# A hybrid attention block on one core: 32 unused bytes ahead of the activations

## The chip, the cores and the metric

The kernel runs on one core of a Trainium2 chip. The time is that of one execution on the device in microseconds; three runs of the kernel before are given by their median, lowest and highest. A profile of one execution stands beside them, with the start and the duration of every instruction.

## What is computed

One decoder block over 512 tokens of width 1024, all in float32, batch 1. Two token mixers run side by side on the same normalised input, their gated results are merged, and a SwiGLU layer follows:

```python
h = rms_norm(x, norm_mix_pre[l])
proj = h @ w_in[l]
(g_q, g_k, g_v, g_r, g_a, n_q, n_kc, n_vc, n_ks, n_vs, n_kw, n_vw,
 n_gate, merge_gla, merge_nsa) = jnp.split(proj, split_points, axis=-1)
o_gla = gla_mixer(g_q, g_k, g_v, g_r, g_a, ...)
o_nsa = nsa_mixer(n_q, n_kc, n_vc, n_ks, n_vs, n_kw, n_vw, n_gate, ...)
mixed = (jax.nn.sigmoid(merge_gla) * (o_gla @ w_proj_gla[l])
         + jax.nn.sigmoid(merge_nsa) * (o_nsa @ w_proj_nsa[l]))
x = x + rms_norm(mixed @ w_out[l], norm_mix_post[l])
h = rms_norm(x, norm_ffn_pre[l])
f = (jax.nn.silu(h @ w_ffn_gate[l]) * (h @ w_ffn_up[l])) @ w_ffn_down[l]
x = x + rms_norm(f, norm_ffn_post[l])
```

`gla_mixer` is a chunked gated linear attention of 4 heads, `nsa_mixer` a sparse attention of 8 heads with a compressed, a selected and a sliding-window branch. The hidden width of the SwiGLU layer is 2816.

## The kernel before

**Products.** Nearly all of the work is dense products of weights with activations that are held transposed, 128 features by 512 tokens to a tile. To keep float32 accuracy at the faster fp32r rate, each operand is split in a high and a low part, both fp32r, and a product is three matmuls into one accumulator: high weights with high activations (line 243), high weights with low activations (line 248), low weights with high activations (line 249). These three lines stand in the helper `three`, which all products with transposed activations share. The weights are the stationary operand, 128x128 to a matmul, and the activations stream past them as the moving operand, so each of the three matmuls has a weight load ahead of it that overlaps with the matmul before (PEld in the profile). The first projection, of line 569, goes the other way: the activations (`hu`) are stationary and the weights move, 440 columns at a time.

**Widths.** Plain products move 512 columns. Pairs of products, and the units of SwiGLU and of the down projection, use a seven-product scheme (as Strassen's) on halves of the tokens and move 256 columns. Line 569 moves 440.

**Stages, in the order of time.** Line 569 projects to the token-major values up to 69 us; then the other projections, woven with GLA, to 245 us; compression and attention with pieces of dense products as filling to 425 us; the output projection to 480 us; SwiGLU to 705 us; the plain part of the down projection to 753 us, the rest of it to the end.

**Where tiles lie.** All on-chip buffers come from pools. A pool of the left side grows upwards from the base, a pool of the right side downwards from the top. The pool `base` is the first on the left: identity, ones, two constants, the norm vectors, then `hT_hi` and `hT_lo` (the activations, 16 KB a partition each) and the eight slots `b0` to `b7`. The other left pools (`mid`, `glat`, `nsa`, `att`, `ffn` and so on) are stacked above it and hold further activations and those weight forms that are sums of weights (`s`, `a22`, the slots `d_two`, `c_two`, `w_uu`, `w_rw` and the like). On the right lie the raw weights as they come from memory (`wraw`) and the ring: two high and two low tiles of 1024 columns, `whi` and `wlo`, through which the other split weights pass, and the softmax tiles. Sizes are rounded up to 32 bytes.

What stands before `hT_hi` adds up to 512 + 512 + 64 + 32 + 32 + 160 = 1312 bytes, 20.5 times 64, from byte 16,512 on, which is 258 times 64. So `hT_hi` starts at byte 17,824, which is 32 mod 64, and since nearly all tiles above it have sizes that are multiples of 128, nearly all of the left side starts at 32 mod 64, as does the right side.

The kernel has earlier devices that set such starts. `half_line` puts 64 bytes into the pool `mid` (line 404), the ring can be opened with a shift of 64 bytes (lines 95 and 131), and the forms of the down projection are shifted by 192 bytes (line 1737). As a result, where 256 columns are moved, the moving operand starts at 32 mod 128 and the weights at 96, 64 bytes apart. Where 512 columns are moved, 613 matmuls with the weights in the ring have both at 32, and 332 have them at 32 and 96. In line 569 the weights move: the two parts of 440 columns in a tile start at 96 and, 1760 bytes further, at 64 mod 128, and the stationary `hu` at 96. Another device is `restart` (line 236), after which the first 256-column product has its middle matmul split in two halves of 128 columns (line 244).

**Order.** Each engine's order follows from the order in which the code issues, and from the waits that the pools set where a buffer is reused. The down projection and the SwiGLU units alternate between weights in the ring and weights in left-side slots.

Of the kernel before, what the change touches and what calls it, by code (L numbers as in the profile page):

```python
# [8 lines left out]
F32 = mybir.dt.float32  # L9
# [141 lines left out]
def hybrid_block_kernel(ctx: ExitStack, tc: tile.TileContext, I, outT):  # L151
# [3 lines left out]
    base = ctx.enter_context(tc.tile_pool(name="base", bufs=1, reuse_waits="tile"))  # L155
# [11 lines left out]
    def bank(tag):  # L167
        return psum.tile([128, 512], F32, tag=tag, bufs=2, name="ps_" + tag)
# [17 lines left out]
    act.activation(out=warm, in_=mhalf[:, 0:1], func=AF.Exp)  # L186
    vecs = base.tile([128, 4 * KD + HG + 2], F32, name="vecs")
    act.dma_start(vecs, I["vecs"])
    spin = bank("acc")
    for i in range(8):  # L190
        pe.matmul(spin[:, 0:128], ones, ones, start=True, stop=True)
# [1866 lines left out]
```

## Time and profile before

| | |
|---|---|
| timed runs | 836.05, 835.23, 834.75 us; median 835.23 us |
| span of the profiled execution, first to last instruction | 833.8 us |
| granted clock of TensorE over the span | 0.997 |
| PE busy | 823.1 us in 5553 matmul records |
| DVE, ACT, POOL busy | 633.1, 526.2, 147.2 us |
| read from and written to memory | 102.21 MB, 4.19 MB |

The profiled execution has no time of its own beside its span; the runs' median lies 1.4 us above the span. How to read the rows: a timeline row gives start and length in us, engine, line, operation, output tile <- input tiles, and the shape. A matmul's recorded length (0.28 us for 256 columns, 0.39 us for 512) includes the time that it takes to pass through the array and overlaps with the next; the step from one start to the next is what a matmul costs in a dense stream.

### The profile page before, as it was taken

The numbers are of one execution on the slowest core, as the hardware profiler recorded it, in microseconds if no ns is written. First come the engines' busy times: TensorE is split into PE (matmuls) and PEld (weight loads), VectorE is DVE, ScalarE is ACT, GpSimd is POOL, SyncE is SP. The second block draws the span as 40 slices with busy tenths as digits, with TensorE's granted clock in tenths as the row PEclk, the third lists the DMA queues.
The fourth block names the chain that finished last, engine by engine and source line by source line (L and its number), as shares of the span: only waits on it lengthen the run. The fifth ranks groups of instructions, "written<-read, shape, count | busy, mean of one in ns | idle before, by whom it ended". The sixth has DMA issues, their size and how long they took to land.

```text
span 833.8 us, 14626 instructions
## 1 busy us (share of the span) xinstructions
PE 823.1 (99%) x5553; PEld 749.7 (90%) x5553; DVE 633.1 (76%) x1198; ACT 526.2 (63%) x973; POOL 147.2 (18%) x176
## 2 busy tenths in 40 slices
PE   9999999999999999999999999999999999999996
PEld 8998899998788787888888999999999999889996
DVE  7765897883377888777666488998888778839985
ACT  6557767763454889887645587766665657535542
POOL 0101022230030000100000365111211110001354
PEclk9999999999999999999999999999999999999998
DMA  8333465762252454454228758789878883325333
GB/s 295 98 110 102 120 121 129 168 145 84 76 182 51 105 127 101 102 127 106 73 76 280 227 153 228 141 209 236 187 187 200 201 182 86 91 77 178 89 103 101
DMA packets 41239, 117.85 MB, mean 141 GB/s; under 512 B 4716, under 2 KB 7036, under 8 KB 41040
## 3 DMA queue, kind: packets, MB, share of 16 engines
q1 hardware_dynamic: 27952, 82.49, 31.9%
q0 software_dynamic: 12496, 33.88, 22.0%
q8 instruction: 43, 0.70, 0.3%
q10 hardware_dynamic: 720, 0.54, 0.2%
q14 instruction: 28, 0.23, 0.1%
HBM read 102.21 MB, written 4.19 MB: 128 GB/s over the span
## 4 chain that ended last, share of the span: by engine, by line
PE 88%; DVE 5%; ACT 4%; POOL 2%; issue 1%; POOLq 0%; DVEq 0%; ACTq 0%
PE ps_mm L243 13%; PE ps_mm L249 13%; PE ps_mm L248 13%; PE ps_sc L243 5%; PE ps_sc L249 5%; PE ps_sc L248 4%; PE ps_acc L248 3%; PE ps_acc L249 3%; PE ps_acc L243 3%; PE ps_tp L249 2%; PE ps_tp L243 2%; PE ps_tp L248 2%; PE ps_tp L569 2%; PE ps_sc L569 2%; PE ps_tp L1139 2%
## 5 line engine op out<-in xcount | busy, mean ns | idle before, releaser
L78 ACT CAST whi<-wraw 128x1024 fp32r<-128x1024 f32 (+2 forms) x62 | 60.2, 973 | 64.9 <-PE ps_mm L248 22.7
L243 PE MATMUL ps_mm<-hT_hi,whi 128*128 128x512 f32 (+1 forms) x260 | 100.1, 385 | 0.2 <-ACT whi L78 0.2
L249 PE MATMUL ps_mm<-hT_hi,wlo 128*128 128x512 f32 (+1 forms) x260 | 97.1, 374 | 0.0
L248 PE MATMUL ps_mm<-hT_lo,whi 128*128 128x512 f32 (+1 forms) x259 | 96.7, 374 | 0.0
L85 DVE TENSOR_TENSOR wlo<-wraw,whi 128x1024 fp32r<-128x1024 f32 (+2 forms) x47 | 51.4, 1096 | 27.0 <-ACT whi L78 26.9
L243 PEld LDWEIGHTS ps_mm<-hT_hi,whi 128*128 128x128 f32 x260 | 48.9, 188 | 10.2 <-ACT whi L78 0.9
L249 PEld LDWEIGHTS ps_mm<-hT_hi,wlo 128*128 128x128 f32 x260 | 48.8, 188 | 9.3 <-DVE wlo L85 0.3
L248 PEld LDWEIGHTS ps_mm<-hT_lo,whi 128*128 128x128 f32 x259 | 48.7, 188 | 7.5
L1462 ACT CAST d_two<-s 128x1024 fp32r<-128x1024 f32 x26 | 27.0, 1044 | 30.5 <-PE ps_mm L249 15.0
L274 DVE TENSOR_TENSOR pl<-ps_tp,ph 128x512 fp32r<-128x512 f32 (+1 forms) x64 | 31.2, 490 | 13.2 <-ACT ph L273 12.5
L1469 DVE TENSOR_TENSOR d_two<-s,d_two 128x1024 fp32r<-128x1024 f32 x25 | 30.6, 1223 | 11.2 <-ACT d_two L1462 10.9
L82 POOL DMA_DIRECT2D wlo<-wraw x15 | 12.8, 852 | 147.3 <-ACT wlo L81 71.3
L1101 ACT ACTIVATE p<-p,mx 128x512 f32<-128x512 f32 (+3 forms) x64 | 35.7, 559 | 4.6 <-DVE mx L1099 4.2
L1099 DVE CUSTOM_DVE_ANT_0 p<-ps_sc,causal 128x512 f32<-128x512 f32 (+3 forms) x64 | 30.0, 488 | 9.5 <-PE ps_sc L1093 8.6
L273 ACT CAST ph<-ps_tp 128x512 fp32r<-128x512 f32 (+1 forms) x64 | 26.6, 417 | 4.4 <-PE ps_tp L1139 3.4
L1838 POOL TENSOR_TENSOR y<-y,us 128x256 f32<-128x256 f32 x12 | 16.0, 1361 | 72.1 <-DVE us L1835 72.1
L1139 PE MATMUL ps_tp<-ident,p 128*128 128x128 f32 x160 | 27.7, 272 | 0.0
L1139 PEld LDWEIGHTS ps_tp<-ident,p 128*128 128x128 f32 x160 | 20.8, 140 | 7.2 <-ACT pc L1023 0.4
L1446 POOL DMA_DIRECT2D wlo<-in_w_gate x13 | 11.5, 887 | 76.8 <-ACT wlo L1444 76.7
L1462 ACT CAST c_two<-s 128x1024 fp32r<-128x1024 f32 x12 | 12.5, 1044 | 18.7 <-PE ps_acc L249 9.5
L243 PE MATMUL ps_mm<-hT_hi,d_two 128*128 128x256 f32 x80 | 22.3, 279 | 0.0
L249 PE MATMUL ps_mm<-hT_hi,d_two 128*128 128x256 f32 x80 | 22.3, 279 | 0.0
(841 smaller groups left out, 3214.6 us busy)
## 6 DMA issues: line engine op xcount, KB each, us to landing
wraw<-in_w_t SPq DMA_DIRECT2D x36, 512.0 KB, 3.9
wraw<-in_w_gate SPq DMA_DIRECT2D x21, 512.0 KB, 4.5
rw<-in_w_up SPq DMA_DIRECT2D x19, 512.0 KB, 8.3
wlo<-wraw POOLq DMA_DIRECT2D x15, 512.0 KB, 4.5
wlo<-in_w_gate POOLq DMA_DIRECT2D x13, 512.0 KB, 8.6
w_uu<-in_w_up POOLq DMA_DIRECT2D x19, 256.0 KB, 8.7
wraw<-in_w_tok SPq DMA_DIRECT2D x11, 440.0 KB, 3.4
wraw<-in_w_proj SPq DMA_DIRECT2D x8, 512.0 KB, 3.6
```

The lines of the kernel that those rows point to most:

```text
L78: self.cast = self.nc.scalar.copy(hi[:, :cols], raw[:, :cols])
L85: self.nc.vector.tensor_tensor(out=lo[:, :cols], in0=raw[:, :cols], in1=hi[:, :cols].bitcast(F32), op=OP.subtract)
L243: pe.matmul(o, wh, xh, start=start, stop=False, skip_group_check=True)
L248: pe.matmul(o[:, c], wh, xl[:, c], start=False, stop=False, skip_group_check=True)
L249: return pe.matmul(o, wl, xh, start=False, stop=stop, skip_group_check=True)
L274: dve.tensor_tensor(out=lo, in0=src, in1=hi.bitcast(F32), op=OP.subtract)
L569: pe.matmul(o, x[:, k, t], y[:, w], start=(k == 0 and m == 0), stop=(k == KD - 1 and m == 2))
L1099: dve.tensor_tensor_reduce(out=o, in0=s, in1=causal[:, S - 128 * (i + 1):S], scale=-1.0, scalar=-NEG, op0=OP.add, op1=OP.min, accum_out=mx ...
L1101: act.activation(out=o, in_=o, func=AF.Exp, scale=-1.0, bias=mx[:, i:i + 1], accum_out=z[:, i:i + 1])
L1139: pe.transpose(tp[:, i * 128:(i + 1) * 128], p[:, OFF[i] + k * 128:OFF[i] + (k + 1) * 128] if i else p0, ident)
L1462: act.copy(hi, t)
L1469: dve.tensor_tensor(out=lo, in0=t, in1=hi.bitcast(F32), op=OP.subtract)
```

## The change

After the norm vectors and ahead of `hT_hi`, one buffer of 8 float32 values a partition is allocated in the pool `base`. Nothing reads or writes it.

```diff
     vecs = base.tile([128, 4 * KD + HG + 2], F32, name="vecs")
     act.dma_start(vecs, I["vecs"])
+    base.tile([128, 8], F32, name="line")
     spin = bank("acc")
```

`hT_hi` starts at byte 17,856 instead of 17,824, and all later left-side tiles move by the same 32 bytes. Their starts of 32 mod 128 become 64, those of 96 become 0. The right side stays where it is, at 32 mod 64. The engines have the same instructions in the same order, with the same waits.

| columns | operands | moving, weights mod 128 before | after | matmuls |
|---|---|---|---|---|
| 256 | both on the left | 32, 96 | 64, 0 | 2116 |
| 256 | moving left, weights in the ring | 32, 96 | 64, 96 | 1222 |
| 512 | moving left, weights in the ring | 32, 32 | 64, 32 | 613 |
| 512 | moving left, weights in the ring | 32, 96 | 64, 96 | 332 |
| 440 | moving in the ring, `hu` on the left | 96, 96 and 64, 96 | 96, 0 and 64, 0 | 288 |

## The prediction

> **What bounds the kernel now.** I read the head of the page first, then the granted clock, then the chain that ended last, and then the starts of single matmuls in the timeline, since the change can only act on how fast an instruction reads or writes its operands.
>
> ```profile
> span 833.8 us, 14626 instructions
> PE 823.1 (99%) x5553; PEld 749.7 (90%) x5553; DVE 633.1 (76%) x1198; ACT 526.2 (63%) x973; POOL 147.2 (18%) x176
> PE 88%; DVE 5%; ACT 4%; POOL 2%; issue 1%; POOLq 0%; DVEq 0%; ACTq 0%
> ```
> ```profile
> core 0: 833.8 us, clock 0.997
> ```
>
> PE is busy for 823.1 of 833.8 us, at a granted clock of 0.997, and it is 88% of the chain. All other waits together leave PE idle for 833.8 - 823.1 = 10.7 us. So the time is the sum of the PE's steps from one matmul to the next, and a change that alters this step by 1% alters the kernel by nearly 1%.
>
> The table by stretches shows that it holds in the two long parts where the other engines have most to do.
>
> ```profile
> 590.00:700.00 110.00, 110.00 (x973) 110.00 (x972) 87.75 (x155) 68.10 (x106) 17.93 (x21) 1.00 0.78 179
> 708.00:752.00 44.00, 44.00 (x191) 35.44 (x190) 28.47 (x44) 22.51 (x39) 0.00 (x0) 1.00 0.27 80
> ```
>
> After the time come PE, PEld, DVE, ACT, POOL, the granted clock, and DMA. In the SwiGLU units (590 to 700) PE has no gap, DVE is busy for 87.75 of 110 us and ACT for 68.10. If PE became 6% faster there, 103.5 us would be left, still more than DVE's 87.75: no other engine would take over.
>
> **The step of a matmul.** The fp32r matmuls have three widths, and the timeline shows what a step of each takes. First 256 columns wide, in one stretch and in another, the first and the last row of 19 each, so 18 steps:
>
> ```profile
> 619.81 0.28 PE L243 MATMUL ps_mm<-x5h,w_uu 128*128 128x256 f32 x1
> ...
> 621.85 0.28 PE L243 MATMUL ps_mm<-x,d_two 128*128 128x256 f32 x1
> ```
> ```profile
> 546.77 0.28 PE L249 MATMUL ps_mm<-x5h,w_uu 128*128 128x256 f32 x1
> ...
> 548.89 0.28 PE L248 MATMUL ps_tp<-hT_lo,d_two 128*128 128x256 f32 x1
> ```
>
> 2.04 us over 18 is 113.3 ns, and 2.12 us over 18 is 117.8 ns. Both stretches have the same starts of their operands (moving at 32, weights at 96 mod 128). So there is a short and a long step, and the start alone doesn't decide which.
>
> Then 512 columns wide, ten rows or nine steps each; in the first pair moving and weights both start at 32 mod 128, in the second the weights start at 96:
>
> ```profile
> 451.73 0.39 PE L248 MATMUL ps_mm<-hT_lo,whi 128*128 128x512 f32 x1
> ...
> 453.77 0.39 PE L248 MATMUL ps_mm<-hT_lo,whi 128*128 128x512 f32 x1
> ```
> ```profile
> 719.76 0.39 PE L243 MATMUL ps_mm<-hT_hi,whi 128*128 128x512 f32 x1
> ...
> 721.86 0.40 PE L243 MATMUL ps_mm<-hT_hi,whi 128*128 128x512 f32 x1
> ```
>
> 2.04 / 9 = 226.7 ns and 2.10 / 9 = 233.3 ns. The first kind isn't always at its best: over the 71 matmuls of w_out's first three tiles and what precedes them on PE (70 steps)
>
> ```profile
> 443.13 0.40 PE L243 MATMUL ps_mm<-hT_hi,whi 128*128 128x512 f32 x1
> ...
> 459.21 0.39 PE L248 MATMUL ps_mm<-hT_lo,whi 128*128 128x512 f32 x1
> ```
>
> the step is 16.08 / 70 = 229.7 ns. Last, the 440 columns of line 569, from the chain in order of time (start, length, what):
>
> ```profile
> 27.48 2.40 PE ps_tp L569 x12
> ...
> 44.28 2.40 PE ps_acc L569 x12
> ```
>
> Twelve matmuls take 2.40 us, 200.0 ns each, in every such group.
>
> These numbers have a common measure. 113.3, 200.0, 226.7 and 233.3 are 17, 30, 34 and 35 times 6.67 ns. Sixteen fp32 columns are 64 bytes, so a step looks like a whole number of slots of 64 bytes: 16 of data and one more for 256 columns, 32 and two or three for 512, and 27.5 and 2.5 for 440. The question of the change is what the additional slots are. A run of 256 columns that starts at 32 mod 64 touches 17 pieces of 64 bytes, and 16 if it starts at 0. That is the hope in it. Line 569 is the one place of the trace where both starts occur: its moving weights are two parts of 440 columns in one tile, the first at 96 mod 128 (32 mod 64), the second 1760 bytes on, at 64 mod 128 (0 mod 64). In each group of 12 half are of one kind and half of the other, and the 2.40 us do not change from group to group whichever the stages do. Each part touches 28 pieces, yet each step costs 30 slots. So two slots have another cause than the start, and if a start at 0 alone made the stream free of them, half of line 569 would show it.
>
> **The change part by part.** (1) The buffer itself: no instruction reads or writes it, so 0 us. The five engines have the same instructions in the same order with the same waits as before; nothing is moved past a queue. (2) Every tile of the left side that follows it starts 32 bytes later; the right side (raw weights, the ring, the softmax tiles) doesn't move.
>
> (3) ACT and DVE on shifted tiles: cost 0. Line 578 writes 440 columns, at 32 mod 64 in the first group (ps_mm, 26.3 us) and at 0 in the second (ps_acc, 46.0 us):
>
> ```profile
> L578 ACT ACTIVATE tok<-ps_mm,rs_x x2: 620/624/627, 26.3 to 26.8; 128x440 f32<-128x440 f32 x2
> ...
> L578 ACT ACTIVATE tok<-ps_acc,rs_x x2: 626/634/642, 46.0 to 47.4; 128x440 f32<-128x440 f32 x2
> ```
>
> 624 against 634 ns is no gain from the start at 0, and both lie under PE's work. DMAs into the left side keep their sizes; PE's whole idle time of 10.7 us bounds what they could give or take.
>
> (4) Matmuls with both operands on the left: 2,116 of 256 columns in the program. Moving goes from 32 to 64 mod 128, weights from 96 to 0: the distance of 64 bytes stays. Bounds: one slot less (-6.7 ns) and the long step (+4.4 ns); I take 0, since line 569 shows no gain from the start and the distance, on which the two kinds of 512 columns differ, is kept.
>
> (5) Moving on the left, weights in the ring: 1,222 of 256 columns, 613 of 512 columns that had the distance 0 and 332 that had the distance 64. All get a distance of 32 bytes, for which no row of such a pair exists. I take the middle of the two steps. For 256 columns, between 113.3 and 117.8: +2.2 ns x 1,222 = +2.7 us. For 512 columns the middle of 226.7 and 233.3 is 230.0: against 229.7 that is +0.3 x 613 = +0.2 us, and against 233.3 it is -3.3 x 332 = -1.1 us. (6) Line 569 turns the other way round, its weights (hu) move and its stream stays: both distances it has had, 0 and 32, give 200.0, so 0.
>
> The sum is 2.7 + 0.2 - 1.1 = +1.8 us on the profiled span of 833.8, so 835.6. The median of the timed runs, 835.23, is 1.4 us above this span, which lies outside the program's own instructions, so I forecast 837.0 us. A measurement of this kernel can tell about 0.2%, or 1.7 us, from no change, so this forecast is at the edge of "same".
>
> A rule of the Trainium skill speaks to item 4. Its page "TensorE: Matmul & The Clock Gate", section "Back-to-back issue gap", gives N/2.4 + 2.5 ns for a warm matmul of N columns, whatever its start: 109.2 ns for 256 and 215.8 ns for 512, an estimate from that page. The rows above (113.3, 226.7 to 233.3) are longer, so it is not the bound here; by that rule no step would depend on where the operands start, and the sum would be 0, 835.2 us.
>
> **The rivals.** (B) The extra slot is the torn piece. For it: 113.3 is exactly the 17 pieces that 256 columns touch from 32 mod 64. Against it: line 569's 30 slots for 28 pieces, and 34 or 35 slots for 512 columns, which touch 33. If it holds, the 3,338 matmuls of items 4 and 5 lose a slot of 6.67 ns, 22.3 us, and 945 of 512 columns lose one each, 6.3 us: at most -28.6 us, 806.6 us. With two thirds of it, because the ring's weights still start at 32, and the phase's +1.8 us, it is about -17 us: 818 us. Its smallest size, half a slot on item 4 alone (3.3 x 2,116), is -7.0 us, or 828.
>
> (C) The other side: the short step of the 256-column matmuls is lost. The two stretches above show that the same starts run at 113.3 and at 117.8, so the step hangs on what went before; the kernel even splits a matmul in two after each restart (line 244). A new distance in the ring's products, which alternate with the left's, could tip the rest. Against it: the distance within item 4 is kept. If all 3,338 went to 117.8 it would be 4.4 x 3,338 = +14.7 us; I take four fifths of it, since stretches like that at 546 us have the long step already: +11.7, or 846.9 us. It decides if the stretch of 590 to 700 us no longer steps at 113.3.
>
> (D) Nothing happens at all: the start within 64 bytes doesn't matter to PE, nor does the distance at 32 bytes, and the time stays at 835.2. For it: line 569. Against it: the two kinds of 512 columns differ by 6.6 ns. Beside it, the Trainium skill's page "SBUF — State Buffer", section "Specifications (TRN2)", gives lines of 16 bytes. A shift by 32 keeps every start at a line, so by that rule nothing would change. That the buffer is dropped can't be: the program places hT_hi at byte 17,856 instead of 17,824.
>
> **How the numbers follow.** A has 0.50, B 0.25, C 0.15, D 0.10. A's own range is 832 to 842: all its pairs at the better of the two rows (113.3, 226.7) give -1.8 - 2.2 = -4.0 us less what is not at its best today, and all at the worse (117.8, 233.3) +5.4 + 2.2 = +7.6. Of A's 0.50, 0.09 is faster by over 0.2%, 0.17 within it and 0.24 slower. B is faster, C slower, D within. That makes faster 0.34, same 0.27, slower 0.39. A and D lie inside 815 to 845; outside are the stronger half of B with about 0.10 and most of C with 0.10, so this is the range. Cases of both signs hold much of the chance, so A's own range stands beside it.
>
> **What would show it.** A is right if the rows at 590 to 700 us still step at 113.3, those at 708 to 752 fall from 233.3 towards 230, and the ring's 256-column products (between 100 and 190 us, and after 755) lengthen by 2 ns. B is right, and my step 4 wrong, if the left's own pairs step below 113, towards 107; line 569 stays at 200.0 then too. C is right if they step at 117.8. If the time moves while all these steps are as before, the cause is one that I have not seen, and the PE's idle 10.7 us is where to look. DVE and ACT durations should not move at all; if they do, step 3 is wrong.

## The result: 0.66% slower, and the profile after

The kernel with the buffer takes 840.71 us (median of 4 runs, 840.40 to 841.62); the kernel before took 835.63 us beside it (4 runs, 834.75 to 836.05). The ratio is 1.0066, with a 95% interval of 1.0053 to 1.0078. The forecast was 837.0 us with a range of 815 to 845, and its case A, a cost in the ring's products, had a range of its own of 832 to 842.

The head of the page of the profile after and its chain by engine (lines of the code are numbered one higher from line 189 on, so `three` has lines 244, 249 and 250):

```profile
span 838.6 us, 14626 instructions
PE 828.8 (99%) x5553; PEld 754.6 (90%) x5553; DVE 633.4 (76%) x1198; ACT 526.4 (63%) x973; POOL 146.3 (17%) x176
PE 90%; ACT 4%; DVE 2%; issue 2%; DMA 1%; POOL 1%; POOLq 0%; ACTq 0%; SPq 0%
```

The span grew by 4.8 us and PE's busy time by 5.7 us; PEld, the weight loads of the same engine, grew by 4.9 us; DVE and ACT are within 0.3 us of before, and POOL is 0.9 us lower. The granted clock is 0.999, against 0.997. So the whole of it lies in PE's steps. The windows that answer to those of before, shifted by the time lost until then:

```profile
593.00:703.00 110.00, 110.00 (x963) 110.00 (x963) 87.13 (x154) 67.29 (x104) 17.88 (x21) 1.00 0.77 178
712.20:756.20 44.00, 44.00 (x190) 35.48 (x190) 28.34 (x43) 22.50 (x39) 0.00 (x0) 1.00 0.27 80
```

PE has no gap in either, as before. In the timeline of the kernel after, four pairs of rows give the steps, each pair the first and the last row of a stretch: w_out's 512 columns (71 matmuls), SwiGLU's pairs on the left side (19 matmuls), the plain down product (10 matmuls), and two products of the down part with their weights in the ring (42 steps, counted from the last matmul of the product ahead of them, whose weights lie on the left).

```profile
445.42 0.39 PE L244 MATMUL ps_mm<-hT_hi,whi 128*128 128x512 f32 x1
...
461.88 0.40 PE L249 MATMUL ps_mm<-hT_lo,whi 128*128 128x512 f32 x1
...
623.08 0.28 PE L244 MATMUL ps_mm<-x5h,w_uu 128*128 128x256 f32 x1
...
625.12 0.28 PE L244 MATMUL ps_mm<-x,d_two 128*128 128x256 f32 x1
...
723.93 0.40 PE L244 MATMUL ps_mm<-hT_hi,whi 128*128 128x512 f32 x1
...
726.03 0.40 PE L244 MATMUL ps_mm<-hT_hi,whi 128*128 128x512 f32 x1
...
761.69 0.28 PE L250 MATMUL ps_sc<-dt,w_g3l 128*128 128x256 f32 x1
...
766.66 0.28 PE L250 MATMUL ps_mm<-dt1e,wlo 128*128 128x256 f32 x1
```

The same two ring products in the timeline of the kernel before:

```profile
757.45 0.28 PE L249 MATMUL ps_sc<-dt,w_g3l 128*128 128x256 f32 x1
...
762.21 0.28 PE L249 MATMUL ps_mm<-dt1e,wlo 128*128 128x256 f32 x1
```

- w_out: 16.46 / 70 = 235.1 ns, before 229.7.
- SwiGLU's left pairs: 2.04 / 18 = 113.3 ns, as before, although both operands now start at 0 mod 64.
- Plain down product: 2.10 / 9 = 233.3 ns, as before.
- Ring products of 256 columns: 4.97 / 42 = 118.3 ns, before 4.76 / 42 = 113.3.

The first projection and its evictions did not move: in the chain of the kernel after the groups of 12 still take 2.40 us, and the evictions last what they did (620/624/627 and 626/634/642 ns before).

```profile
27.52 2.40 PE ps_tp L570 x12
...
44.32 2.40 PE ps_acc L570 x12
```
```profile
L579 ACT ACTIVATE tok<-ps_mm,rs_x x2: 619/623/627, 26.3 to 26.9; 128x440 f32<-128x440 f32 x2
L579 ACT ACTIVATE tok<-ps_acc,rs_x x2: 627/636/645, 46.0 to 47.5; 128x440 f32<-128x440 f32 x2
```

**The sum by kind.** The order of PE's instructions is the same in both kernels, so each matmul can be set against itself. The table gives the difference of its step (from its start to the next one's) between the two traces, added up over each kind. The kinds are told apart here by the name of the weights' tile and by time, so the counts differ somewhat from those by start in the table of the change:

| kind | matmuls | mean step before and after, undisturbed ones | sum |
|---|---|---|---|
| 256 columns, weights `whi` or `wlo` in the ring | 1,236 | 114.5, 118.4 ns | +3.6 us |
| 512 columns, weights in the ring, 190 to 465 us (for the most part starts 32 and 32 before) | 792 | 229.8, 232.8 ns | +1.9 us |
| 512 columns, weights in the ring, up to 107 us and from 700 us (starts 32 and 96 before) | 288 | 233.3, 233.3 ns | 0.0 us |
| 256 columns, weights in slots on the left | 2,035 | 114.2, 114.3 ns | -0.4 us |
| all matmuls | 5,553 | | +4.8 us |

(Undisturbed leaves out steps in which PE also waited, those above 135 ns for 256 columns and above 250 ns for 512. Steps with waits that became shorter gave 1.1 us of the first kind back, and the -0.4 us of the fourth and another -0.4 us of all other matmuls are mostly of this sort too.)

### The profile page after: what moved, and what is told of

It is laid out like the page before. It is cut to its first block, busy times and chain, and to the rows that moved or that the text cites. A ratio compares the mean times of both kernels' runs of the same rounds, so it can differ in the third digit from the quotient of the medians.

```text
span 838.6 us, 14626 instructions
## 1 busy us (share of the span) xinstructions
PE 828.8 (99%) x5553; PEld 754.6 (90%) x5553; DVE 633.4 (76%) x1198; ACT 526.4 (63%) x973; POOL 146.3 (17%) x176
## 4 chain that ended last, share of the span: by engine, by line
PE 90%; ACT 4%; DVE 2%; issue 2%; DMA 1%; POOL 1%; POOLq 0%; ACTq 0%; SPq 0%
PE ps_mm L244 14%; PE ps_mm L250 13%; PE ps_mm L249 13%; PE ps_sc L244 5%; PE ps_sc L250 5%; PE ps_sc L249 5%; PE ps_acc L250 3%; PE ps_acc L249 3%; PE ps_acc L244 3%; PE ps_tp L250 3%; PE ps_tp L244 3%; PE ps_tp L249 3%; PE ps_tp L570 2%; PE ps_sc L570 2%; PE ps_tp L1140 2%
```

## The experiments

Two theories stood against each other. The distance theory: what counts is where the weights of a matmul start relative to its moving operand, and the buffer moved one of the two for the ring's products. The start theory: a start of 0 mod 64 on the left side costs in itself. A third possibility was that the long step is only a matter of what ran before. In what follows d is the start of the weights less the start of the moving operand, mod 256.

### Move both, move the other, move twice as far

The ring's place is set by the openings of its pool (before and after: 0, 16 and 0 floats). The first kernel keeps the buffer and moves the ring by the same 32 bytes mod 128 (openings 24, 40, 24):

```diff
-    wts.open(0)
+    wts.open(24)
...
-            self.pool.open(16)
+            self.pool.open(40)
```

> The 32 bytes stay, and the ring's split weights move by the same 32 bytes mod 128 (the ring is opened with shifts of 24, 40 and 24 floats instead of 0, 16 and 0). All operands of the dense products then start at 0 mod 64, and every distance between moving operand and weights is that of the kernel before. If the distance alone counts: 835 to 836 us, as before; ring products of 256 columns back at a step of 113 to 115 ns, those of 512 columns at 229 to 230. If the start at 0 mod 64 on the left side costs: 840 to 841 us, as with the change. If a start at 0 helps and only the ring's odd start hid it: below 832 us.

Measured: 836.48 us (835.49 to 837.94, 11 runs), a ratio of 1.0017 (1.0008 to 1.0026) to before. The second has no buffer and moves the ring alone (openings 8, 24, 8):

```diff
-    base.tile([128, 8], F32, name="line")
-    wts.open(0)
+    wts.open(8)
...
-            self.pool.open(16)
+            self.pool.open(24)
```

> The kernel before, without the 32 bytes; only the ring's weights move, by 32 bytes mod 128 (shifts 8, 24, 8). The left side keeps its starts at 32 mod 64, and the ring's products get a distance of 32 bytes, as with the change. If the distance counts: 840 to 841 us. If the start of the left side counts: 835 to 836 us.

Measured: 840.55 us (840.05 to 841.55, 5 runs), ratio 1.0066 (1.0052 to 1.0079). The third doubles the buffer:

```diff
-    base.tile([128, 8], F32, name="line")
+    base.tile([128, 16], F32, name="line")
```

> The unused buffer has 64 bytes instead of 32. The left side starts at 32 mod 64 again, but the ring's products of 256 columns have the distance 0 (96 and 96 mod 128), and those of 512 columns swap: the 613 get 64, the 332 get 0. If the distance counts: 256 columns at 118 ns, +4 x 1222 = +5 us; 613 x +3.6 ns = +2.2 us; 332 x -3.6 = -1.2 us: about 841 to 842 us. If only the start mod 64 counts: 835 to 836 us.

Measured: 844.31 us (843.93 to 844.67, 4 runs), ratio 1.0112 (1.0098 to 1.0125). The same two ring products in the three timelines, with both moved,

```profile
757.96 0.28 PE L250 MATMUL ps_sc<-dt,w_g3l 128*128 128x256 f32 x1
...
762.72 0.28 PE L250 MATMUL ps_mm<-dt1e,wlo 128*128 128x256 f32 x1
```

with the ring alone moved,

```profile
762.79 0.28 PE L249 MATMUL ps_sc<-dt,w_g3l 128*128 128x256 f32 x1
...
767.76 0.28 PE L249 MATMUL ps_mm<-dt1e,wlo 128*128 128x256 f32 x1
```

and with 64 bytes:

```profile
765.27 0.28 PE L250 MATMUL ps_sc<-dt,w_g3l 128*128 128x256 f32 x1
...
770.31 0.28 PE L250 MATMUL ps_mm<-dt1e,wlo 128*128 128x256 f32 x1
```

4.76, 4.97 and 5.04 us over 42 steps are 113.3, 118.3 and 120.0 ns. With both moved, moving and weights start at 64 and 0 mod 128 and have the short step; with the ring alone moved, nothing on the left side starts at 0 mod 64, and the loss of the change is there in full, +3.6 and +2.0 us by kind (beside one wait of 0.7 us in SwiGLU). The start theory is refuted, and the distance theory holds for the ring's products. Why the kernel with both moved still takes 1.3 us more than before shows in the section on the period.

With 64 bytes something else shows that no theory had foreseen. The pairs on the left keep their distance there, yet SwiGLU's run at 117.8 ns, and the left pairs cost 4.8 us more than before. The same timeline, at the first units, shows how it comes about:

```profile
562.53 0.28 PE L244 MATMUL ps_mm<-hT_hi,d_two 128*128 128x256 f32 x1
...
563.56 0.28 PE L244 MATMUL ps_sc<-x4h,whi 128*128 128x256 f32 x1
...
564.88 0.28 PE L250 MATMUL ps_sc<-x4h,wlo 128*128 128x256 f32 x1
...
624.45 0.28 PE L250 MATMUL ps_sc<-x4h,wlo 128*128 128x256 f32 x1
...
627.28 0.28 PE L250 MATMUL ps_mm<-x,d_two 128*128 128x256 f32 x1
```

After the split of a matmul at 562.19 us the left pairs take 1.03 / 9 = 114.4 ns; then come twelve ring products at 1.32 / 11 = 120.0, and the left pairs after such a group have the long step, here 2.83 / 24 = 117.9 (rows 4 and 5), up to the end of the units. The same pairs with the same starts have both steps within one run, so the distance alone doesn't decide. That the ring products at 120.0 ns between them bring the long step is the likely reading of these rows; no run tests it by itself.

### A map by itself, first attempt

A benchmark of matmuls alone, without the block: 16 pairs of starts, 256 and 512 columns (an excerpt of the program).

```diff
...
+            for j, (w, x) in enumerate(((wh, xh), (wh, xl), (wl, xh))):
+                chain(ps[:, 0:n], w[:, c], x[:, a], start=(q == 0 and j == 0),
+                      stop=(q == TRIPLES - 1 and j == 2), skip_group_check=True)
...
```

> The step measured by itself: the kernel leaves out the whole block and returns x with 128 columns overwritten. It runs stretches of 48 matmuls in threes (high weights with high and with low activations, low weights with high activations), 256 and 512 columns wide, for the 16 combinations of a start at 0, 32, 64, 96 mod 128 of the moving operand (letters a to d after m) and of the weights (after s), each twice, the second time in reverse order. If the distance alone counts, the four combinations of one distance have one step: at 256 columns 113.3 ns for 64 apart and 117 to 119 for 0 and 32 apart; at 512 columns 227 to 230 for 0 apart, 232 to 234 for the others. If the start counts, rows of m differ whatever s is: m at a and c shorter than b and d by up to 6.7 ns if torn pieces of 64 bytes cost. If neither counts, all steps agree within 1 ns.

Inconclusive for 256 columns: no stretch of it came down to 113.3 ns, not even at the starts at which the kernel has it; the last 30 steps of a stretch had means of 116.7 to 120.9 (without the first stretch, whose first matmuls took 213 ns). Its 512 columns had 231.1 or 233.3. It split no matmul, and its pairs were told apart mod 128 only, which the next runs showed to be too coarse. By the tile sizes in its program (16,512 bytes for the activations, 4,224 for the weights) the low tiles also start 128 bytes away from the high ones mod 256, so every product mixed two distances, such as 64 and 192.

### The two terms apart

The changed kernel with the ring moved (openings 24, 48, 24) so that its 256-column products are 64 bytes mod 128 from their moving operand again, but those of w_out (the middle opening) are not:

```diff
-    wts.open(0)
+    wts.open(24)
...
-            self.pool.open(16)
+            self.pool.open(48)
```

> The changed kernel with the ring's tiles moved as well, so that its weights of 256-column products start at 0 and their distance to the moving operand (64) is 64 bytes again, as before; the weights of w_out's 512-column products go back to 32, so their distance stays 32 bytes, as in the changed kernel. Distance theory: the 256-column ring products return from 118.3 to 113.3 to 115.3 ns (about -3.4 us), the other 512-column ones fall from 233.2 to 229.3 (-1.3 us), w_out stays near 232.7: about 836.2 us. Rival, the start at 0 mod 64 itself costs: nothing changes, 840.7 us.

Measured: 836.71 us (836.20 to 837.48, 11 runs), ratio 1.0020 (1.0012 to 1.0029). The counterpart gives only the 512-column products of the middle opening their distance back (openings 0, 8, 0):

```diff
-            self.pool.open(16)
+            self.pool.open(8)
```

> The changed kernel with only the middle opening of the ring moved by 32 bytes, so that the 512-column products of GLA's projections and of w_out have moving operand and weights at the same distance (0 mod 256) as in the kernel before; the ring's 256-column products and the other 512-column ones stay 32 bytes nearer, as in the changed kernel. The counterpart of the kernel that gave the 256-column products their distance back. If the two terms are apart and add, the stretch of w_out falls from 235.0 to 229.7 ns or less and only the 512-column term goes: 840.7 - 1.9 = 838.8 us, with the ring's 256 columns still at 118.3 ns. Rival, the 512-column step hangs on what went before and not on the distance: w_out stays at 235, 840.7 us.

Measured: 839.09 us (838.51 to 840.11, 5 runs), ratio 1.0050 (1.0037 to 1.0064). Its timeline in w_out (70 steps) and in the ring products (42 steps):

```profile
444.17 0.40 PE L244 MATMUL ps_mm<-hT_hi,whi 128*128 128x512 f32 x1
...
460.27 0.39 PE L249 MATMUL ps_mm<-hT_lo,whi 128*128 128x512 f32 x1
...
761.00 0.28 PE L250 MATMUL ps_sc<-dt,w_g3l 128*128 128x256 f32 x1
...
765.97 0.28 PE L250 MATMUL ps_mm<-dt1e,wlo 128*128 128x256 f32 x1
```

16.10 / 70 = 230.0 ns and 4.97 / 42 = 118.3 ns: w_out is back where it was before, the ring is not. By kind against before, the sum of the second kind, which holds w_out, is 0.0 us, and that of the ring's 256 columns is still +3.7 us beside one wait of 0.7 us. Against the kernel before, run beside each, the change costs 5.1 us, this kernel 4.2 us and the one with the 256 columns given back 1.3 us. So the 256-column term is seen in the times too. The 512-column term of 0.9 us is not clear of their intervals of about 1 us either way and rests on the steps. In the kernel with the 256 columns given back, 1.2 us came from the third kind, which fell from 233.3 to 229.0 ns.

### The period

By the distance mod 128 that third kind should not have fallen, since it had 64 bytes before as well. A buffer of 128 bytes keeps every start mod 128:

```diff
-    base.tile([128, 8], F32, name="line")
+    base.tile([128, 32], F32, name="line")
```

> An unused buffer of 128 bytes in place of 32: every start of the left side is as in the kernel before mod 128, but 128 bytes later. If only starts mod 128 matter, every step is as before: 835.2 us within 0.2%. If the period is longer, 256 bytes for instance, distances are off by half of it and the ring products lengthen as they did with 64 bytes: 840 to 844 us.

Measured: 836.07 us (835.18 to 837.02, 11 runs), ratio 1.0009 (1.0000 to 1.0018). The time is that of before within 0.2%, but the steps are not. Its timeline from the first matmul of the plain down product to the one behind its last, 192 steps:

```profile
709.63 0.39 PE L244 MATMUL ps_mm<-hT_hi,whi 128*128 128x512 f32 x1
...
753.58 0.28 PE L244 MATMUL ps_sc<-db,whi 128*128 128x256 f32 x1
```

43.95 / 192 = 228.9 ns in place of 233.3, while w_out went from 229.7 to 234.5. By kind that is -1.2 and +1.3 us, which cancel. Only the distance mod 256 changes here, for these pairs from 64 to 192 and from 0 to 128. The expectation's longer period was right, its time wrong: at half of 256 the 256-column pairs keep the short step.

It also explains the 1.3 us of the first kernel with both moved. Mod 256 its distances are not those of before: its ring products of 256 columns have d = 192 and the short step, and w_out has d = 128. In its timeline w_out takes

```profile
444.08 0.39 PE L244 MATMUL ps_mm<-hT_hi,whi 128*128 128x512 f32 x1
...
460.55 0.40 PE L249 MATMUL ps_mm<-hT_lo,whi 128*128 128x512 f32 x1
```

16.47 / 70 = 235.3 ns, about as long as with the change (235.1).

### The map again, mod 256

The benchmark once more, leaving out the block, with eight distances and with a split in one of two 256-column stretches (an excerpt).

```diff
...
+                two = split and q == 2 and j == 1
+                for o in (0, 128) if two else (0,):
+                    e = 128 if two else n
...
```

> A benchmark of matmuls alone, which leaves out the block: stretches of 60 matmuls, three to a product as in the kernel, the moving operand at one start and the weights 0 to 224 bytes on in steps of 32, each distance with 256 columns unsplit, with 256 columns and a split in the third product, and with 512 columns; everything twice, the second time in the reverse order. Distance and memory: after a split the distances of 64, 128 apart (64 and 192) stay at 113.3 ns, the others go to 117.8 to 120; unsplit stretches start in the long step and stay there. 512 columns: 226.7 to 229 at 0, 233 and over at 32 and 128. Rival, the step is set by what goes before alone: split stretches take 113.3 at every distance.

Two stretches with a split, d = 64 and d = 192 (31 rows each, so 30 steps, from the timeline):

```profile
88.37 0.28 PE L47 MATMUL split_wc<-xh,wl 128*128 128x256 f32 x1
...
91.77 0.28 PE L47 MATMUL split_wc<-xh,wl 128*128 128x256 f32 x1
...
204.37 0.28 PE L47 MATMUL split_wg<-xh,wl 128*128 128x256 f32 x1
...
207.90 0.28 PE L47 MATMUL split_wg<-xh,wl 128*128 128x256 f32 x1
```

3.40 / 30 = 113.3 and 3.53 / 30 = 117.7 ns. And an unsplit stretch at d = 64 in the second pass:

```profile
398.65 0.28 PE L47 MATMUL whole_wc_again<-xh,wl 128*128 128x256 f32 x1
...
402.18 0.28 PE L47 MATMUL whole_wc_again<-xh,wl 128*128 128x256 f32 x1
```

3.53 / 30 = 117.7 ns, where the first pass had 113.3 at the same distance. The mean of the last 30 steps for every distance, over both passes and both ways of 256 columns, beside the kernels' own stretches (the ring products after 757 us, w_out's 71 matmuls, the plain down product; w_out's means hold a slow start of some 14 matmuls, 1.7 to 3 ns):

| d | map, 256 columns | map, 512 columns | kernels, 256 in the ring | kernels, w_out | kernels, plain down |
|---|---|---|---|---|---|
| 0 | 120.0 | 226.7 | 120.0 (64 bytes) | 229.7 (before) | 226.8 (64 bytes) |
| 32 | 118.2 to 118.5 | 233.3 | 118.3 (after) | | 233.4 (after) |
| 64 | 113.3 or 117.8 | 233.3 | 113.3 (before) | | 233.3 (before) |
| 96 | 117.3 to 118.7 | 234.3 | | 236.0 (ring's 256 columns given back) | |
| 128 | 118.7 | 233.3 | | 234.5 (128 bytes), 235.3 (both moved) | |
| 160 | 120.0 | 233.3 | | | |
| 192 | 113.3 or 117.8 | 228.9 | 113.3 (128 bytes, both moved) | 231.4 (64 bytes) | 228.9 (128 bytes, both moved) |
| 224 | 116.5 to 116.8 | 233.3 to 233.4 | | 235.1 (after) | |

Once the slow start is left out of w_out's means, the map reproduces the kernels' steps within 1 ns by the distance mod 256. In the map only the weights move; that their own start is not the cause is shown by the kernels above in which the left side moved instead. At 64 and 192 two steps are possible, and only there the short one. What chooses is not shown: the unsplit stretches at both distances changed over between the passes, in which different stretches run ahead of them, and with a split it was 113.3 at 64 and 117.8 at 192 both times. That a split always brings the short step, as both theories had it, is wrong, and so is the expectation that stretches without a split stay in the long one.

### No split, and more splits

The kernel before without the split of line 244; the order of the instructions changes in places.

```diff
-        cut = [slice(0, 128), slice(128, 256)] if fresh[0] and n == 256 else [slice(0, n)]
+        cut = [slice(0, 128), slice(128, 256)] if False else [slice(0, n)]
```

> The kernel before without any split of a matmul after a restart; all starts as before. The scheduler changes the order in a few places. If the split is what brings the short step, the SwiGLU units run at 117.8 in place of 113.3: 3,300 matmuls x 4.4 = +14 us less 0.5 for the splits saved, up to 849 us. If the distance of 64 bytes alone gives the short step, whatever went before: 835 us or a little less.

> The same program without splits once more, for a profile: its executions took 835.3 to 843.0 us, and the one profiled was among the short ones, with 113.3 ns in the units. Memory of the step: an execution of 841 us or more shows the units or the down part at 117.8 ns with the same starts and the same order; if the time moves without that, the memory is not what separates the executions.

Measured: a median of 841.06 us with executions from 835.30 to 842.98 (12 runs), ratio 1.0054 (1.0034 to 1.0074), and 837.26 in one more run. Neither expected time came. The units ran at 113.3 ns in both profiles, so the first theory's price of +14 us is wrong. What is long in both are the left pairs behind w_out, here from the timeline of the later run (40 rows), and then the same stretch of the kernel before, behind its split (41 rows):

```profile
460.12 0.28 PE L243 MATMUL ps_sc<-hT_hi,w_rw 128*128 128x256 f32 x1
...
464.72 0.28 PE L243 MATMUL ps_sc<-hT_hi,w_uu 128*128 128x256 f32 x1
```
```profile
460.60 0.28 PE L248 MATMUL ps_sc<-hT_lo,w_rw 128*128 128x256 f32 x1
...
465.13 0.28 PE L249 MATMUL ps_sc<-hT_hi,w_uu 128*128 128x256 f32 x1
```

4.60 / 39 = 117.9 ns without the split, and 4.53 / 40 = 113.3 ns with it. Both profiled executions were among the short ones (836.69 and 837.26), so what separates them from those of 841 to 843 us was not seen.

Two attempts at a faster kernel. The first, from the kernel before, moves the activations of the plain down product by 64 bytes (d = 0) and adds two splits. The room for the move is made where `hT_hi` and `hT_lo` are allocated, as in the second attempt below, with 16 floats in place of 32:

```diff
...
-    fh, fl = (lambda k: hT[:, k, :]), (lambda k: hTl[:, k, :])
+    fh, fl = (lambda k: hTd[:, k, :]), (lambda k: hTld[:, k, :])
...
-        if j == 0:
+        if j in (0, 19):
             restart()
...
+        if n == N0:
+            restart()
         product(r1, "a12", "b21", False)
```

> The kernel before with three edits of its own. The activations of the plain down product start at 96 instead of 32 (192 matmuls of 512 columns, distance 0 to their weights in place of 64), and two more matmuls are split in two after a place where the step had become the long one: ahead of the product a12 of the first Strassen unit, and ahead of the 20th product of the down part. Theory of distance and memory: the down product falls from 233.3 to 227.3 ns (192 x 6.0 = -1.15 us), some 230 matmuls between 531 and 557 us and some 190 between 799 and 822 us fall from 117.8 to 113.3 (-1.0 and -0.85 us), each split costs 0.11 us: 832.4 us. Rival, a split doesn't set the step, only what follows does: -1.15 + 0.22, 834.3 us. Rival, the start itself matters and not the distance: the down product stays at 233.3.

Measured: 842.19 us (842.00 to 842.48, 4 runs), ratio 1.0086 (1.0073 to 1.0099), against 832.4 expected. The down product fell to 226.8 ns as forecast. The loss is in the units, here 35 steps from its timeline:

```profile
609.00 0.28 PE L243 MATMUL ps_tp<-hT_hi,d_two 128*128 128x256 f32 x1
...
613.12 0.28 PE L249 MATMUL ps_acc<-hT_hi,d_two 128*128 128x256 f32 x1
```

4.12 / 35 = 117.7 ns in place of 113.3. The room for the moved activations had shifted `hT_lo` and all later tiles by 128 bytes, but not `hT_hi`. All starts mod 128 are as before, which was thought to be enough; mod 256 the left pairs are not: those with `hT_hi` moving have d = 192 now, those with `hT_lo` still 64, and they alternate within a product. In the units as a whole (525 to 707 us) the matmuls that move `hT_hi` past `d_two` or `c_two` have medians of 118 ns and those that move `hT_lo` 117 ns, while those that move `x5h` or `x`, all with d = 64, have 113 ns. So here a mixture of the two good distances went with the long step. The second leaves out that first split and moves the down product's activations by 128 bytes (d = 192), with all other starts unchanged mod 256:

```diff
-    hT = base.tile([128, KD, S], F32R, name="hT_hi")
-    hTl = base.tile([128, KD, S], F32R, name="hT_lo")
+    hroom = [base.tile([128, KD * S + 32], F32R, name=n) for n in ("hT_hi", "hT_lo")]
+    (hT, hTd), (hTld, hTl) = [[x[:, c:c + KD * S].rearrange("p (k t) -> p k t", k=KD) for c in (0, 32)] for x in hroom]
...
-    rs_x = base.tile([128, 64], F32, name="rs_x")[:, 0:NT]
+    rs_x = mhalf[:, 12:12 + NT]
...
```

> The kernel before with the activations of the plain down product alone moved by 128 bytes (192 matmuls of 512 columns: distance to their weights 64 in place of 192 mod 256; four columns of norm scales move into another buffer so that nothing else shifts) and a second split of a matmul ahead of the 20th product of the down part. If the distance mod 256 sets the 512-column step, the down product falls from 233.3 to the 228.9 ns that the buffer of 128 bytes gave (192 x 4.4 = -0.85 us), and the split brings 117.8 to 113.3 after 799 us (-0.75 us net): about 833.7 us. Rival, the step follows only what went before: the down product stays at 233.3, 834.5 us; and a way into the long step in the units, as in the version with three edits, would give 841.

(That text counts the distance the other way round, from the weights to the moving operand: its 192 and 64 are d = 64 before and d = 192 now.) Measured: 834.90 us (833.42 to 836.14, 11 runs), ratio 0.9999 (0.9990 to 1.0008). Its timeline, 192 steps of the down product and 42 of ring products behind the added split:

```profile
708.25 0.40 PE L243 MATMUL ps_mm<-hT_hi,whi 128*128 128x512 f32 x1
...
752.21 0.28 PE L243 MATMUL ps_sc<-db,whi 128*128 128x256 f32 x1
...
801.32 0.28 PE L249 MATMUL ps_mm<-hT_lo,w_g3l 128*128 128x256 f32 x1
...
806.08 0.28 PE L249 MATMUL ps_sc<-dt3e,wlo 128*128 128x256 f32 x1
```

43.96 / 192 = 229.0 ns and 4.76 / 42 = 113.3 ns (117.8 before): both steps fell as forecast. `hT_lo` starts a whole 256 bytes later here than before, and the units that use it keep 113.3 ns from 570 us on, which agrees with a period of 256. The profiled span is 833.1 us, 0.7 us below that of before, and the timed runs can't tell it from before. No kernel was shown to be faster than the one before.

## Why the prediction was right, and where its sizes were wrong

The forecast's case was A, a cost in the products that have one operand on each side, and that is what happened; 840.7 us lies in A's own range of 832 to 842. What was right is which kinds pay and which do not. The time says less: the whole range of 815 to 845 is 30 us wide, A's own holds gains as well as losses, and slower had a chance of 0.39 against 0.34 for faster, so the sign was hardly forecast. The point value of 837.0 was 3.7 us too low, for the most part because the terms of step 5 were mis-sized. By its steps:

1. Buffer and order: right. No engine but PE changed by 1 us.
2. Step 3, ACT and DVE at no cost: right (623 and 636 ns against 624 and 634).
3. Step 4, left pairs at no cost: right, 113.3 ns in the rows, and 114.2 before against 114.3 after over the undisturbed 256-column matmuls with weights on the left. Its reason, the kept distance, is not enough by itself, since with 64 bytes the same pairs lost the short step at a kept distance; so this was in part luck. Rival B is refuted: both operands start at 0 mod 64 there, and the step is not below 113 ns. The slots of 6.67 ns behind it hold for 113.3, 120.0, 226.7 and 233.3 ns, but 117.8, 118.3 and 228.9 ns are no whole number of them.
4. Step 5, the ring's 256 columns: direction right, size wrong. The prediction took the middle of the two steps, +2.2 ns; measured is +3.9 ns for the undisturbed ones and, with shorter waits in it, +3.6 us in place of +2.7. There is no middle: at a distance of 32 the short step isn't reached, and the map has 118.2 to 118.5 there in all four stretches. By the step the worse row (+4.4 ns) was nearer than the middle; in the sum its +5.4 us was not, because the kernel's own mean was 114.5 and not 113.3 before, and waits became shorter.
5. Step 5, the 613 matmuls at distance 0: +0.3 ns was taken, +3.0 measured, +1.9 us in place of +0.2. This is the larger error, 1.7 us. The dense part of w_out, behind its first 14 matmuls, stepped at 226.7 before and steps at 233.3 now; the 229.7 of before was a mean over a slow start and a short step, and the prediction treated it as the height of the step itself.
6. Step 5, the 332 at distance 64: a gain of 1.1 us was taken, none came (0.0 us). The prediction took a distance of 32 to lie between the short step at 0 and the long one at 64. The map has 233.3 at 32 and at 64; short are only 0 and 192.
7. Step 6, line 569: the result is right, 2.40 us for twelve. The reason given covers half of it: mod 128 its distances go from 0 and 32 to 32 and 64, and 64 had not been seen there before.

With the measured terms the sum would have been 3.6 + 1.9 + 0.0 = +5.5 us; waits that became shorter elsewhere took 0.8 us off, and +4.8 was measured over all matmuls. What failed was interpolation between two rows, three times: each time a step between the two was taken, and about the long one or a longer one came.

Rival C, the loss of the short step in the left pairs, didn't happen here, where the units stay at 113.3 ns, but it is real: with 64 bytes it cost 4.8 us, at unchanged distances, behind ring products at 120.0 ns. At 32 bytes, behind ring products at 118.3 ns, it did not happen; why is not shown. Rival D is refuted by the result, and its reason, that line 569 is indifferent, doesn't carry over to the products of 256 and 512 columns.

Two rules of the Trainium skill bear on the cause. Its page "SBUF — State Buffer", section "SBUF: two separate sides", says that PE never waits on another reader; this agrees, since the loss appears without any change on the other engines, but the weights' place relative to PE's own moving operand is worth 5.0 ns on 113.3 here. The page "TensorE: Matmul & The Clock Gate" says in "Back-to-back issue gap" that in a stream of weight loads and matmuls both set the spacing. The run with the ring alone is in line with that: the step goes from 113.3 to 118.3 ns when only the weights move. That the weight load and the stream meet in the same piece of memory is a possible reading of a period of 256 bytes, but no run here shows the mechanism.

Open stay two things: what decides between 113.3 and 117.8 ns at distances 64 and 192, and why executions of the kernel without splits differ by up to 7.7 us.

## What to carry to other kernels

In a kernel bound by dense fp32r matmuls, a buffer that nobody uses can cost more than half a per cent, because it moves one operand of a matmul against the other; before a pool is changed, list the starts of moving operands and weights mod 256 by kind of matmul, and keep their distance. Where two rows show a short and a long step, don't take the middle for a case in between: price it at either end. A step that has two values at the same starts can also turn a whole stage whose own starts kept their distance, as with 64 bytes, so the stages behind an edit are to be read again.

## What was not expected of the hardware

- The step of a dense fp32r matmul follows the distance of its operands' starts mod 256: at 256 columns 113.3 ns is reached only at 64 and 192, and 116.5 to 120 elsewhere; at 512 columns 226.7 ns at 0, 228.9 at 192, and 233.3 to 234.3 elsewhere. At distance 0 the 512 columns have their best step and the 256 columns their worst.
- At 64 and 192 the stream has two lasting steps, 113.3 and 117.8 ns, and can stay in one of them for a whole stage: in the run with 64 bytes the long one lasted from 564 us to the end of the units.
- The absolute start within 64 bytes showed no effect: pairs with both operands at 0 mod 64 in place of 32 step at 113.3 ns again, on the left side and in the ring.
